# The crossing between two layers: token rows modulated in place and transposed by DMA instead of by TensorE

## The chip, the cores and the metric

The kernel runs on one core of a Trainium2 chip. Its five engines run from queues of their own and meet through semaphores: TensorE (PE, with its weight loads shown as PEld), VectorE (DVE), ScalarE (ACT), GpSimd (POOL) and SyncE (SP), whose queue issues most of the DMAs; ScalarE and GpSimd issue a few as well. The metric is the device time of one execution in microseconds. The kernel before takes 1306.46 us, the median of three runs (1306.09 to 1312.27).

## The reference, cut to what matters

One step of a two-layer backbone on 256 context ("prompt") tokens and 1024 latent tokens of width 1024. Layer 0 mixes tokens by a chunked gated linear attention (GLA), layer 1 by grouped-query softmax attention. Each layer normalises, scales and shifts its input, and adds its gated branch to it:

```
h = rms_norm(x, norm_g[l]) * (1 + sc) + sh        # sc, sh, gt: of the request, by silu(c) @ w_ada[l] + b_ada[l]
# layer 0
y = (rms_norm(o_f + flip(o_b), onorm) * silu(gate)) @ w_out
x = x + gt * y
# layer 1
q, k, v, gate = split(h @ w_in)                   # on the new x, normalised and modulated for layer 1
q = rms_norm(q, qn); k = rms_norm(k, kn)          # latent tokens: rope_2d(q), rope_2d(k)
```

Context and latent tokens have different sc, sh and gt. All products are formed in 16 bits with each factor split into a high and a low half (three products for one), so each h is needed as hi and lo, with the width on the partitions.

## The kernel before, in words

The tokens are ten tiles of 128: tiles 0 and 1 are the prompt, 2 to 9 the latent tokens. `hT_hi` and `hT_lo` hold the 16-bit halves of a layer's input, transposed: width on the partitions, tokens along the free dimension.

The GLA layer is a loop of 50 slots (`gla`): four heads over ten tiles, and ten more slots in which the last head is finished. A function `filler(slot)` hangs other work on the slots: the products with `w_ada`, the splitting of layer 1's weights, the layer's scale and shift (`affine(1)` in slot 37), the loading of w_out (slots 30 to 38). Work that shall wait for the slot's own instructions is put into `k.jobs` and run under `issue_after`. In slots 42, 44, 46 and 48 the gated outputs of tiles 2 to 5 are split and transposed by DMA into `hT` (`out_load`, `out_prep`); in slots 45 and 47 the first two output tiles are multiplied (`residual` with the banks A and kt).

`gla_out` is the crossing: it carries the tiles from layer 0 to layer 1, in the order 2 to 9, 0, 1. For each tile n from the third on: load the tile's row x, multiply the gated output with w_out (`residual`: two halves of 512 columns, each in a PSUM bank "y"; VectorE scales the bank by the gate and adds it into x), store x for the next layer (`x1_d`, by GpSimd's queue), split and transpose the gated output of the tile after next. After every second tile both x are normalised (`normalise`: squares summed by ScalarE, the power -1/2 by GpSimd, the row scaled by VectorE). While the next pair is multiplied, the finished pair is transposed by TensorE, 128 columns at a time, into PSUM banks "tr" (`transpose`); ScalarE applies scale and shift from there (`modulate`, `h`), GpSimd rounds to `hT_hi`, VectorE writes the rest to `hT_lo`. Then the pair's two key tiles are multiplied (`key_tile`, banks "kv"), normed, turned by the rotary table and transposed by DMA into `kT`. After the loop the rotary table is multiplied with the query norm (`fold_rope`), the query weights are loaded (`query_start`), two query tiles are projected, and the last pair, the prompt, is transposed and modulated. The prompt's own key tiles come in `attention`, between the score products (bank S) of its first step.

The program says what depends on what and which tile has how many buffers. The order of instructions on each engine and queue is made by the framework, which plays the program through with modelled durations and issues what is ready first; `issue_after(x)` puts a group behind instruction x on x's engine. On the chip each engine and queue then keeps that order. DMAs that transpose are all issued from SP.

Of the kernel before, what the change touches and what calls it, by code (L numbers as in the profile page):

```python
# [7 lines left out]
F16 = mybir.dt.float16  # L8
BF16 = mybir.dt.bfloat16
F32 = mybir.dt.float32  # L10
# [43 lines left out]
class K:  # L54
# [269 lines left out]
    def affine(self, l):  # L324
        nc, sp = self.nc, self.const
        mod = self.modT[l]
        g = self.t(sp, [P, KT, 2], F32, f"gs{l}")
        gT = self.gT[:, 8 * l : 8 * l + 8].unsqueeze(2).to_broadcast([P, KT, 2])
        nc.vector.scalar_tensor_tensor(g, mod[:, 8:16, :], 1.0, gT, ALU.add, ALU.mult)
        sh = self.t(sp, [P, KT, 2], F32, f"sh{l}")  # L330
# [10 lines left out]
        return g, sh, c  # L341
# [432 lines left out]
    def residual(self, i, lhs, wo, inv, x, banks=None, cuts=(512, 512), out=None):  # L774
        nc = self.nc
        g = self.gt[:, 0 if i < NTP else 1, :]
        b = 0
        for j, n in enumerate(cuts):
            ps = (banks[j] if banks else self.bank("y"))[:, 0:n]
            self.pieces(ps, lhs, wo, b, n)  # L780
            a = slice(b, b + n)
            nc.vector.scalar_tensor_tensor(ps, ps, inv, g[:, a], ALU.mult, ALU.mult)  # L782
            last = nc.vector.tensor_tensor(x[:, a], ps, x[:, a], ALU.add).ins  # L783
# [7 lines left out]
    def out_load(self, i, og=None, parts=None):  # L791
        if og is None:
            og = self.t(self.xp, [P, D], F32, "og", bufs=2)
            t = self.t(self.xp, [P, 2 * D], F16, "oghl", bufs=2)
            parts = t[:, 0:D], t[:, D:]
        self.nc.sync.dma_start(og, self.og_d[i])
        return i, og, parts

    def out_prep(self, i, og, parts):
        nc = self.nc  # L800
        mx = self.t(self.small, [P, 1], F32, "wm1")
        nc.vector.tensor_reduce(mx, og, AX.X, ALU.max, apply_absolute_value=True)
        s, inv = self.pow2(mx, cross=False)
        hi, lo = parts
        nc.scalar.activation(hi, og, AF.Copy, scale=s)
        nc.vector.scalar_tensor_tensor(lo, og, s, hi, ALU.mult, ALU.subtract)
        to = [t[:, :, i * P : i * P + P] for t in (self.hT_hi, self.hT_lo)]
        nc.sync.dma_start_transpose(to[0], hi)
        nc.sync.dma_start_transpose(to[1], lo)
        return *to, inv  # L810


    def gla_out(self, wo, early, first):
# [3 lines left out]
        done, xs = (order[0], first), []  # L817
        self.gs, self.sh, self.inv_h = self.mod1
        rows = {n: self.out_load(order[n]) for n in range(len(early), len(first) + 4)}
        ckv = self.att_load()  # L820
        for n in range(len(first), NT):
            i = order[n]
            hT, lT, inv = prep.pop(i)
            x = self.t(self.xp, [P, D], F32, "xr", bufs=4)
            nc.sync.dma_start(x, xrow(self.I, i))
            last = self.residual(i, lambda k: (hT[:, k, :], lT[:, k, :]), wo, inv, x)
            nc.gpsimd.dma_start(self.x1_d[i], x)
            with self.tc.issue_after(last):
                if n + 2 in rows:
                    prep[order[n + 2]] = self.out_prep(*rows.pop(n + 2))  # L830
            if n + 4 in range(len(early), NT):
                rows[n + 4] = self.out_load(order[n + 4])
            if done:
                t0, ys = done
                if i % 2 == 0:
                    for k in range(KT):
                        act, dve = self.modulate(self.transpose(ys, k, "tr"), k, t0)
                else:
                    for j in range(2):
                        self.key_tile(t0 + j, wkv)  # L840
                    done = None
            xs.append(x)
            if n == len(first):
                d, inv = self.ahead["kv"]
                wkv = []
                t = self.w2[1]
                for j, (hi, lo) in enumerate((
                    [t[:, :, 256:512] for t in self.nw[0:2]], (t[:, :, 0:256], t[:, :, 256:512])
# [5 lines left out]
                with self.tc.issue_after(dve.ins):  # L854
                    self.att_setup(*ckv)
                    self.key_setup(*ckv, inv)
            if i % 2 == 1:
                junk = self.t(self.xp, [P, D], F16, "junk", bufs=1)
                self.normalise(xs, junk)
                done, xs = (i - 1, xs), []  # L860
# [78 lines left out]
    def att_load(self):  # L939
# [4 lines left out]
        nc.sync.dma_start(self.qn, I["att_qnorm"].to_broadcast([P, HD]))  # L944
        self.kn = self.t(ap, [P, HD], F32, "kn")
        nc.sync.dma_start(self.kn, I["att_knorm"].to_broadcast([P, HD]))
# [88 lines left out]
    def queries_out(self, q, j):  # L1035
# [4 lines left out]
        if i >= NTP:  # L1040
            r = self.head_rms(x)
            self.rope(x, i)
        else:
            self.head_norm(x, self.qn, x)
        self.split_transpose(x, None, qT[:, j].rearrange("p i h t -> p (i h) t"), r)
# [79 lines left out]

    def query_start(self):
        d, inv = self.ahead.pop("q0")
        lo = self.t(self.wp, [P, KT, 512], F16, "wlo0")
# [3 lines left out]
        self.wg = [self.load_w("g0", (0, 2))]  # L1132
# [5 lines left out]
        self.q, self.half = {}, []  # L1138

# [113 lines left out]
def emit(ctx, tc, I, O, dbg=None, stop=None):  # L1253
# [15 lines left out]
    k.gt_d = k.t(k.dram, [2, 2, D], F32, "gt_d")  # L1269
    hp = k.pool("hp")  # L1270
# [11 lines left out]
    with ExitStack() as c:  # L1282
# [8 lines left out]
        with ExitStack() as c1:  # L1291
# [51 lines left out]
            k.gs, k.sh, k.inv_h = k.affine(0)  # L1343
# [41 lines left out]
        def filler(slot):  # L1385
# [13 lines left out]
            if slot == 37:  # L1399
                k.mod1 = k.affine(1)  # L1400
# [15 lines left out]
            if slot == 40:  # L1416
                k.jobs.append((k.fold_gate, *k.gate_load(0), [t[2] for t in wo]))
                wo[:] = [(*k.w0[0:2], 512)] + [(hi, lo, 256) for hi, lo, _ in wo[2:]]
                k.w2 = k.wtile(2)
                t = k.w2[0].rearrange("p k n -> p (k n)").bitcast(F32)  # L1420
                for n in range(2):
                    xs.append(t[:, D * n : D * n + D])
                    load(xs[n], xrow(I, NTP + n))
            if slot in PREP:
# [5 lines left out]
            if slot in EARLY:  # L1430
# [6 lines left out]
                if n == 1:  # L1437
                    k.jobs.append((k.normalise, xs, k.t(k.qkp, [P, 512], F32, "q0").bitcast(F16)))
# [7 lines left out]
    with ExitStack() as ca:  # L1446
        k.ap = k.pool("ap", ctx=ca, side="right")
        with ExitStack() as c:
# [4 lines left out]
            k.held = {t: k.bank(t) for t in ("y", "kv", "tr", "mm")}  # L1453
            k.p2_bank = "kv"
            wk = k.gla_out(wo, prep, xs)
# [109 lines left out]
```

## Time and profile before

| | |
|---|---|
| median of 3 runs | 1306.46 us |
| profiled execution, its own time | 1307.08 us |
| its span, first to last instruction | 1305.2 us |
| mean granted TensorE clock | 0.984 |
| busy: PE, DVE, ACT, POOL | 1222.4, 907.5, 713.3, 370.9 us |
| GLA layer with its filler | 0 to 581 us |
| crossing (first y product to first score product) | 581.27 to 737.51 us |
| attention | 737.51 to about 1207 us |
| last output product | to 1305.2 us |

In the profile a line such as "L129 PE MATMUL y<-whi,hT_hi" names the line of the kernel, the engine, the operation, the tile written and the tiles read; L129 is the helper that forms all three-product matmuls, so the tile written tells which stage it is: y an output tile, kv a key tile, mm a query, gate or value product, S scores, tr a transpose (L358). PE instructions are pipelined, so the time that one takes is read from start to start, and the printed duration is longer. The rows themselves are shown with the prediction.

### The profile page before, as it was taken

What the parts mean: (1) busy time and instruction counts of PE and PEld (TensorE: products, weight loads), DVE (VectorE), ACT (ScalarE), POOL (GpSimd) and SP (SyncE); (2) the same over time, 40 slices, a digit from 0 to 9 for tenths busy, and PEclk for the clock granted to TensorE, in tenths of its full rate; (3) what the DMA queues carried; (4) which work ended last, traced back from release to release, by engine and by line L of the source; (5) the groups of instructions that cost most, each with busy time, mean ns of one, the idle gap of its engine ahead of it and who ended that gap; (6) DMA issues with size and microseconds to landing.
All of it is one profiled execution on the core that took longest, in us unless ns stands there. A gap on an engine that the chain in (4) does not pass through costs nothing. (4 is left out here: it accounts for less than half of the span.)

```text
span 1305.2 us, 22423 instructions
## 1 busy us (share of the span) xinstructions
PE 1222.4 (94%) x8015; PEld 791.3 (61%) x8015; DVE 907.5 (70%) x2110; ACT 713.3 (55%) x1730; POOL 370.9 (28%) x625
## 2 busy tenths in 40 slices
PE   4899999999998998798999889999999999989998
PEld 2366666555655556566877466667666666766444
DVE  5585879777876798666664667777667577786652
ACT  3684656565655566542443566666766677673110
POOL 1132214323322244311332643342233344322000
PEclk8899999999999999899999999999999999999999
DMA  9602745554646344257643376666947747879342
GB/s 366 245 33 82 219 149 179 168 158 130 189 139 195 116 150 142 82 150 261 162 120 108 91 179 130 126 131 133 202 105 167 141 87 145 175 151 236 126 153 81
DMA packets 335792, 199.12 MB, mean 153 GB/s; under 512 B 229838, under 2 KB 320446, under 8 KB 333376
## 3 DMA queue, kind: packets, MB, share of 16 engines
q1 hardware_dynamic: 328512, 180.79, 52.9%
q0 software_dynamic: 3728, 11.55, 2.7%
q10 hardware_dynamic: 3440, 5.35, 1.1%
q8 instruction: 63, 1.03, 0.3%
q14 instruction: 49, 0.40, 0.1%
HBM read 104.31 MB, written 37.24 MB: 108 GB/s over the span
## 5 line engine op out<-in xcount | busy, mean ns | idle before, releaser
L129 PEld LDWEIGHTS <-hT_hi 128*128 128x128 f16 x1920 | 188.7, 98 | 126.3 <-issue 12.8
L129 PE MATMUL mm<-whi,hT_hi 128*128 128x512 f16 (+1 forms) x576 | 200.6, 349 | 5.5 <-ACT gx L526 4.8
L129 PE MATMUL mm<-whi,hT_lo 128*128 128x512 f16 (+1 forms) x576 | 200.7, 348 | 0.0
L129 PE MATMUL mm<-wlo,hT_hi 128*128 128x512 f16 (+1 forms) x576 | 200.7, 348 | 0.0
L1094 DVE SCALAR_TENSOR_TENSOR phl<-p,srec,phl 128x1280 f16<-128x1280 f32 (+1 forms) x80 | 108.0, 1355 | 74.3 <-POOL phl L1091 43.5
L129 PEld LDWEIGHTS <-whi 128*128 128x128 f16 x1232 | 120.5, 98 | 61.6 <-issue 3.1
L129 PE MATMUL mm<-hT_hi,whi 128*128 128x256 f16 (+1 forms) x480 | 141.3, 294 | 0.7 <-ACT rope L1014 0.7
L129 PE MATMUL mm<-hT_lo,whi 128*128 128x256 f16 (+1 forms) x480 | 141.3, 294 | 0.0
L129 PE MATMUL mm<-hT_hi,wlo 128*128 128x256 f16 (+1 forms) x480 | 141.2, 294 | 0.0
L1061 PE MATMUL S<-kT,wst 128*128 128x512 f16 (+1 forms) x624 | 124.7, 342 | 11.5 <-ACT p L1069 11.5
L129 PEld LDWEIGHTS <-hT_lo 128*128 128x128 f16 x960 | 94.5, 98 | 61.6 <-issue 1.4
L129 PE MATMUL mm<-PT,vh 128*128 128x256 f16 x672 | 113.8, 275 | 8.8 <-DMA PT<-phl 6.0
L1091 POOL TENSOR_SCALAR phl<-p,srec 128x1280 f16<-128x1280 f32 (+1 forms) x40 | 55.4, 1384 | 200.4 <-DVE srec L1085 74.2
L1064 DVE TENSOR_REDUCE smx<-S 128x1 f32<-128x1280 f32 (+1 forms) x80 | 101.5, 1268 | 11.7 <-PE S L1061 11.7
L1069 ACT ACTIVATE p<-S,snb,sexp 128x1280 f32<-128x1280 f32 (+1 forms) x80 | 99.3, 1242 | 8.6 <-DVE phl L1094 3.7
L1061 PEld LDWEIGHTS <-wst 128*128 128x128 f16 x624 | 61.6, 99 | 66.1 <-issue 15.6
L129 PE MATMUL mm<-PT,vl 128*128 128x256 f16 x336 | 92.3, 275 | 0.0
L152 DVE TENSOR_REDUCE wmx<-wst 128x1 f32<-128x512 f32 x104 | 64.7, 676 | 22.0 <-DMA wst<-in_gla_w_in 8.7
L129 PEld LDWEIGHTS <-wlo 128*128 128x128 f16 x616 | 60.3, 98 | 31.5 <-DVE wlo L1222 1.8
L129 PEld LDWEIGHTS <-vh 128*128 128x128 f16 x672 | 65.6, 99 | 19.9 <-issue 8.3
L1066 ACT ACTIVATE snb<-smx,nsexp 128x1 f32<-128x1 f32 x80 | 23.3, 291 | 85.0 <-DVE smx L1064 84.8
L901 POOL TENSOR_TENSOR rope<-hx,ropet 128x64 f32<-128x64 f32 x160 | 63.1, 424 | 18.8 <-ACT hx L1027 11.2
(358 smaller groups left out, 2724.2 us busy)
## 6 DMA issues: line engine op xcount, KB each, us to landing
wada<-in_w_ada SPq DMA_DIRECT2D x16, 1024.0 KB
wst<-in_gla_w_in SPq DMA_DIRECT2D x12, 1024.0 KB
wst<-in_att_w_in SPq DMA_DIRECT2D x10, 1024.0 KB
og_d<-gx SPq DMA_DIRECT2D x40, 128.0 KB
og_d<-og POOLq DMA_DIRECT2D x40, 128.0 KB, 2.8
wst<-og_d SPq DMA_DIRECT2D x5, 1024.0 KB
xr<-x_d SPq DMA_DIRECT2D x9, 512.0 KB
out<-xr ACTq DMA_DIRECT2D x17, 256.0 KB
```

The lines of the kernel that those rows point to most:

```text
L129: self.nc.tensor.matmul(out, a, b, start=k == 0 and j == 0, stop=k == n - 1 and j == 2)
L152: nc.vector.tensor_reduce(mx[:, j : j + 1], st[:, 2 * j : 2 * j + 2, :], AX.XY, ALU.max, apply_absolute_value=True)
L901: nc.gpsimd.tensor_tensor(tv[:, h, :, w, :], xv[:, h, :, 1 - w, :], sn[:, :, w, :], ALU.mult)
L1061: nc.tensor.matmul(S[:, a : a + n], x, y, start=m == 0, stop=m == 2)
L1064: last = nc.vector.tensor_reduce(mx, S, AX.X, ALU.max).ins
L1066: nc.scalar.activation(nb, mx, AF.Copy, scale=self.nsexp)
L1069: nc.scalar.activation(p, S, AF.Exp, scale=self.sexp, bias=nb, accum_out=den)
L1091: nc.gpsimd.tensor_scalar(hi, p, r, 2.0 ** 14, ALU.mult, ALU.mult)
L1094: nc.vector.scalar_tensor_tensor(lo, p, r2, hi, ALU.mult, ALU.subtract)
```

## The change

The modulated rows are formed with tokens on the partitions and then transposed by DMA.

- `affine(1)` writes scale and shift into one tile. It runs as a job of slot 34. A job of slot 35 (`affine_rows`) transposes this tile on TensorE into 32 rows, copies them out of PSUM and stores them as `gb_d` in DRAM. `rows_load` loads scale and shift of one request, each 1024 values, broadcast to all partitions: 512 KB each, for the latent tokens in slot 40, for the prompt before tile 0.
- `mod_tile` replaces `normalise`, `transpose` and `modulate` for a tile: squares on ScalarE, the power on GpSimd, x times the factor times the scale row on VectorE, plus the shift row in two halves, rounding to `hi` on ScalarE, the rest to `lo` on VectorE, and two transposing DMAs of 128 x 1024 into `hT`. The first two tiles have it as jobs of slots 45 and 47, the others directly behind their residual.
- There is no "tr" bank; "y" has four buffers instead of two, and the PSUM banks are taken in the order kv, mm, y.
- Key tiles come one by one: none with the first output tile of `gla_out`, one with the next, then two, then one each; the last latent key tile and the two query tiles stand ahead of the last output tile.
- The first two query tiles are normed with `qn` itself and turned by the unfolded table; the table is folded after the loop (`query_low`). The low half of the first query weights is loaded into the place of `og` for them, and once more into its old place `wlo0` afterwards.
- The second half of the key weights goes into a tile of its own (`half`). The x rows are loaded two tiles ahead, the first two of them by GpSimd's queue, and so are the two norm vectors.

```diff
     def affine(self, l):
...
-        g = self.t(sp, [P, KT, 2], F32, f"gs{l}")
+        gb = self.t(sp, [P, 2, 2, KT], F32, f"gb{l}")
+        g, sh = (gb[:, j].rearrange("p i k -> p k i") for j in range(2))
...
+    def affine_rows(self, gb):
+        ps = self.bank("mm")[0:32, 0:P]
+        self.nc.tensor.transpose(ps, gb.rearrange("p s i k -> p (s i k)"), self.ident)
+        r = self.t(self.ew, [P, 256], F32, "mod")[0:32, 0:P]
+        self.nc.vector.tensor_copy(r, ps)
+        self.nc.sync.dma_start(self.gb_d.rearrange("s i (k p) -> (s i k) p", p=P), r)
+
+    def rows_load(self, i):
+        t = self.gb.rearrange("p k n -> p (k n)").bitcast(F32)
+        self.gbr = [t[:, D * j : D * j + D] for j in range(2)]
+        for j in range(2):
+            self.nc.sync.dma_start(self.gbr[j], self.gb_d[j, i : i + 1, :].to_broadcast([P, D]))
+
+    def mod_tile(self, i, x, parts, after=None):
...
+        nc.scalar.activation(hi, x, AF.Square, accum_out=ssq)
+        r = self.rstd(ssq, D, "nt_r")
+        g, b = self.gbr
+        with ExitStack() as c:
+            if after is not None:
+                c.enter_context(self.tc.issue_after(after))
+            nc.vector.scalar_tensor_tensor(x, x, r, g, ALU.mult, ALU.mult)
+            cuts = [slice(512 * j, 512 * j + 512) for j in range(2)]
+            for a in cuts:
+                nc.vector.tensor_tensor(x[:, a], x[:, a], b[:, a], ALU.add)
+            for a in cuts:
+                nc.scalar.copy(hi[:, a], x[:, a])
+                nc.vector.tensor_tensor(lo[:, a], x[:, a], hi[:, a], ALU.subtract)
+        for t, p in ((self.hT_hi, hi), (self.hT_lo, lo)):
+            nc.sync.dma_start_transpose(t[:, :, i * P : i * P + P], p)
...
-            ps = (banks[j] if banks else self.bank("y"))[:, 0:n]
+            ps = (banks[j] if banks else self.bank("y", 4))[:, 0:n]
...
-    def gla_out(self, wo, early, first):
+    def gla_out(self, wo, early, n0):
...
+        def load(n):
+            if n < NT:
+                xs[n] = self.t(self.xp, [P, D], F32, "xr", bufs=4)
+                (nc.gpsimd if n < n0 + 2 else nc.sync).dma_start(xs[n], xrow(self.I, order[n]))
+
+        load(n0)
+        load(n0 + 1)
...
+        for n in range(n0, NT):
             i = order[n]
+            if n == NT - 1:
+                self.query_rest()
+                self.query()
+                self.key_tile(order[n - 2], wkv)
+                self.query_rest()
...
+            load(n + 2)
...
-            if done:
-                t0, ys = done
-                if i % 2 == 0:
-                    for k in range(KT):
-                        act, dve = self.modulate(self.transpose(ys, k, "tr"), k, t0)
-                else:
-                    for j in range(2):
-                        self.key_tile(t0 + j, wkv)
-                    done = None
-            xs.append(x)
+            t = self.t(self.xp, [P, 2, D], F16, "hl", bufs=2)
+            if i == 0:
+                self.rows_load(0)
+            self.mod_tile(i, x, (t[:, 0], t[:, 1]), self.last)
+            for j in {3: (0,), 4: (1, 2), 5: (3,), 6: (4,), 7: (5,), 8: (6,)}.get(n, ()):
+                self.key_tile(order[j], wkv)
+            if n == 8:
+                self.query()
...
-        self.fold_rope(self.qn)
-        self.query_start()
-        for j in range(2):
-            self.query()
-            self.query_rest()
-        t0, ys = done
-        for k in range(KT):
-            self.modulate(self.transpose(ys, k, "tr"), k, t0)
+            if n == 7:
+                self.query_start()
+        self.query_low()
...
+    def query_low(self):
+        self.fold_rope(self.qn)
+        self.folded = True
+        d, inv = self.ahead.pop("q0")
+        lo = self.t(self.wp, [P, KT, 512], F16, "wlo0")
+        self.nc.sync.dma_start(lo, d[:, 1])
+        self.wq = [((self.q0, lo, inv), self.wq[0][1])]
+        self.wg = [self.load_w("g0", (0, 2))]
...
-            if slot == 37:
-                k.mod1 = k.affine(1)
+            if slot == 34:
+                k.jobs.append((lambda: setattr(k, "mod1", k.affine(1)),))
+            if slot == 35:
+                k.jobs.append((k.affine_rows, k.mod1[0]))
...
-                if n == 1:
-                    k.jobs.append((k.normalise, xs, k.t(k.qkp, [P, 512], F32, "q0").bitcast(F16)))
+                t = k.t(k.spl, [P, 2, KT // 2, 256], F16, "split").rearrange("p j k n -> p j (k n)")
+                k.jobs.append((k.mod_tile, NTP + n, xs[n], (t[:, 0], t[:, 1])))
...
-            k.held = {t: k.bank(t) for t in ("y", "kv", "tr", "mm")}
+            k.held = {t: k.bank(t, n) for t, n in (("kv", 2), ("mm", 2), ("y", 4))}
```

More of the change, by code (lines that the diff above doesn't have):

```diff
@@ L853, in gla_out @@
                     wkv.append((hi, lo, 256))
-                with self.tc.issue_after(dve.ins):
+                with self.tc.issue_after(last):
                     self.att_setup(*ckv)
                     self.key_setup(*ckv, inv)
[L857 to L860, printed above, removed]
             if n == 4:
@@ L1039, in queries_out @@
         r = None
-        if i >= NTP:
+        if i >= NTP and self.folded:
             r = self.head_rms(x)
@@ L1044, in queries_out @@
             self.head_norm(x, self.qn, x)
+            if i >= NTP:
+                self.rope(x, i)
         self.split_transpose(x, None, qT[:, j].rearrange("p i h t -> p (i h) t"), r)
@@ L1126, in query_start @@
     def query_start(self):
-        d, inv = self.ahead.pop("q0")
-        lo = self.t(self.wp, [P, KT, 512], F16, "wlo0")
+        self.folded = False
+        d, inv = self.ahead["q0"]
+        lo = self.og.rearrange("p j n -> p (j n)").bitcast(F16).rearrange("p (k n) -> p k n", k=KT)
         self.nc.sync.dma_start(lo, d[:, 1])
```

44 lines of the change are left out of this document (24 added, 20 removed).

## The prediction, made before the result was known

> **What bounds the kernel now.** I read the busy time by stretches first, then the TensorE's timeline through the crossing, then what the other engines do beside it. The stretches (columns: length, then busy time and count of PE, PEld, DVE, ACT, POOL, the granted clock, the DMA share, GB/s):
>
> ```profile
> core 0: us, PE busy (x) PEld busy (x) DVE busy (x) ACT busy (x) POOL busy (x), PEclk, DMA share, GB/s
> 581.27:737.51 156.24, 148.22 (x1095) 108.30 (x1092) 95.54 (x234) 62.55 (x156) 47.84 (x107) 0.98 0.53 156
> 737.51:1207.50 469.99, 448.68 (x3186) 312.17 (x3185) 333.22 (x649) 308.50 (x747) 162.96 (x249) 0.99 0.72 149
> 1207.50:1305.20 97.70, 91.17 (x445) 43.10 (x443) 45.36 (x76) 8.86 (x8) 0.54 (x1) 1.00 0.34 120
> ```
>
> The crossing is the first row: PE is busy 148 of 156 us, no other engine more than 96. So the stage costs what PE has to do in it, plus the few places where PE stands. The timeline of PE shows both (start, duration, and in brackets the idle time before with its releaser):
>
> ```profile
> 581.27 0.38 PE L129 MATMUL y<-whi,hT_hi 128*128 128x512 f16 x1
> ...
> 591.69 0.60 PE L358 MATMUL tr<-ident,whi 128*128 128x128 f32 x4
> 595.99 0.58 PE L129 MATMUL y<-whi,hT_hi 128*128 128x512 f16 x1 [3.70 <-DVE xr L783]
> ...
> 602.05 0.60 PE L358 MATMUL tr<-ident,whi 128*128 128x128 f32 x4
> 602.48 0.38 PE L129 MATMUL y<-whi,hT_hi 128*128 128x512 f16 x1
> ...
> 616.94 0.27 PE L129 MATMUL kv<-whi,hT_hi 128*128 128x256 f16 x1
> ...
> 627.42 0.27 PE L129 MATMUL y<-whi,hT_lo 128*128 128x256 f16 x1
> ...
> 729.51 0.60 PE L358 MATMUL tr<-ident,xr 128*128 128x128 f32 x4
> 731.86 0.89 PE L358 MATMUL tr<-ident,xr 128*128 128x128 f32 x4 [1.74 <-ACT h L370]
> 733.82 0.44 PE L358 MATMUL tr<-ident,xr 128*128 128x128 f32 x2 [1.07 <-ACT h L370]
> 735.68 2.03 PE L358 MATMUL tr<-ident,xr 128*128 128x128 f32 x6 [1.43 <-ACT h L370]
> 737.51 2.56 PE L1061 MATMUL S<-kT,wst 128*128 128x512 f16 x9
> 739.91 0.38 PE L129 MATMUL mm<-whi,hT_hi 128*128 128x512 f16 x1
> ...
> 745.09 1.79 PE L1061 MATMUL S<-kT,wst 128*128 128x512 f16 x9
> 746.71 0.27 PE L129 MATMUL mm<-whi,hT_hi 128*128 128x256 f16 x1
> ```
>
> From start to start: a whole output tile (y) is 591.69 - 581.27 = 10.42 us; two key tiles are 627.42 - 616.94 = 10.48, so 5.24 each; a query projection (24 products of 512 columns) is 745.09 - 739.91 = 5.18, or 0.216 a product; four transposes are 602.48 - 602.05 = 0.43. Two places are lost time. At 592 PE waits 3.70 us for a y bank, and the 21 products behind it then take 602.05 - 595.99 = 6.06 instead of 4.53: 1.5 more at a lower clock. At the end the prompt tiles' 16 transposes last from 729.51 to 737.51, 8.0 us, because each waits for ScalarE to empty a tr bank; and the first S group after them takes 739.91 - 737.51 = 2.40 where the next takes 1.62, another 0.8.
>
> [...]
>
> **The change, part by part.** Removed from PE: 64 transposes among the output tiles, 16 x 0.43 = 6.9; the tail, 8.0 with its own 16; the slow first S, 0.8. Two changes lift the wait at 592: four y banks instead of two, so that PE may go on while VectorE is late, and the x row begun on the GpSimd queue, because the lateness was this:
>
> ```profile
> 589.19 0.75 DVE L782 SCALAR_TENSOR_TENSOR y<-y,p2i,wst 128x512 f32<-128x512 f32 x1
> 595.24 0.69 DVE L783 TENSOR_TENSOR xr<-y,xr 128x512 f32<-128x512 f32 x1 [5.30 <-DMA xr<-in_x_sample]
> 588.89 0.42 SPq L825 DMA_DIRECT2D xr<-in_x_sample  x1
> ```
>
> The row was issued at 588.89, behind everything else on SP, and landed 6.35 us later. Either change alone lifts PE's wait: 3.7 + 1.5 = 5.2. Together 6.9 + 8.0 + 0.8 + 5.2 = 20.9. As a check the other way round: eight y tiles, eight key tiles and two queries are 83.4 + 41.9 + 10.4 = 135.7 us of PE, so S could begin at 581.27 + 135.7 = 717.0 instead of 737.5, 20.5 earlier, and 0.8 more for the first S. I take 21.
>
> What replaces them goes to VectorE, ScalarE and the SP queue. The prices, from the groups of instructions of the crossing (busy and mean ns, then idle before):
>
> ```profile
> L375 DVE TENSOR_TENSOR hT_lo<-h,hT_hi 128x256 f16<-128x256 f32 x37 | 15.4, 443 | 6.4 <-POOL hT_hi L374 6.4
> L782 DVE SCALAR_TENSOR_TENSOR y<-y,p2i,wst 128x512 f32<-128x512 f32 x16 | 12.1, 756 | 16.1 <-PE y L129 16.1
> L783 DVE TENSOR_TENSOR xr<-y,xr 128x512 f32<-128x512 f32 x16 | 11.0, 685 | 5.4 <-DMA xr<-in_x_sample 5.3
> L806 DVE SCALAR_TENSOR_TENSOR oghl<-og,p2s,oghl 128x1024 f16<-128x1024 f32 x6 | 7.7, 1283 | 2.7 <-ACT oghl L805 2.6
> L802 DVE TENSOR_REDUCE wm<-og 128x1 f32<-128x1024 f32 x6 | 7.2, 1207 | 0.0
> L352 DVE TENSOR_SCALAR xr<-xr,nt_r 128x1024 f32<-128x1024 f32 x8 | 6.0, 751 | 4.1 <-DMA x_d<-xr 2.5 <-POOL nt_r L120 1.5
> L903 DVE TENSOR_TENSOR hx<-hx,ropet 128x256 f32<-128x256 f32 x12 | 5.4, 453 | 7.4 <-POOL rope L901 7.4
> L890 DVE SCALAR_TENSOR_TENSOR hx<-hx,hrs,kn 128x128 f32<-128x128 f32 x16 | 4.9, 349 | 6.3 <-POOL hrs L120 6.3
> L936 DVE SCALAR_TENSOR_TENSOR xhl<-hx,asc,xhl 128x256 f16<-128x256 f32 x8 | 3.9, 492 | 0.9 <-ACT xhl L935 0.9
> L1010 DVE SCALAR_TENSOR_TENSOR vl<-kv,psv,vh 128x256 f16<-128x256 f32 x8 | 3.9, 482 | 3.4 <-ACT vh L1009 3.4
> L910 DVE TENSOR_TENSOR ropet<-ropet,qn 128x1024 f32<-128x1024 f32 x1 | 1.2, 1212 | 0.0
> L98 DVE TENSOR_SCALAR p2e<-p2c 128x1 int32<-128x1 int32 x6 | 0.9, 152 | 0.2
> ```
>
> - A token tile's modulation cost VectorE 0.75 + 4 x 0.44 = 2.5 us; now one 1024-wide product (1.28), two 512-wide sums and two 512-wide differences (4 x 0.685): 4.0. With the residual (2 x 1.44 = 2.9), the next tile's split (1.21 + 1.28 + 4 x 0.15 = 3.1) and a key tile (0.48 + 2 x 0.35 + 2 x 0.45 + 0.49 + 0.15 = 2.7) VectorE has 12.7 us per tile against PE's 10.42 + 5.24 = 15.7. It stays beside PE; if that cover went, each us over 15.7 would cost 8. ScalarE and GpSimd lose work (no 256-wide copies out of tr banks, no hT_hi copies), and have more room still.
> - SP gets two more transposing DMAs per tile, beside the two of the split. It held them like this, and a store of x delayed the write in place like this:
>
> ```profile
> 601.33 1.32 SPq L808 DMA_TRANSPOSE hT_hi<-oghl  x1
> 602.75 1.59 SPq L809 DMA_TRANSPOSE hT_lo<-oghl  x1
> 650.50 0.75 DVE L352 TENSOR_SCALAR xr<-xr,nt_r 128x1024 f32<-128x1024 f32 x1 [1.48 <-DMA x_d<-xr]
> 702.97 0.33 SPq L1129 DMA_DIRECT2D wlo<-w_q  x1
> ```
>
> The next two rows are a stretch (same columns as above) and PE in the last GLA slots:
>
> ```profile
> 710.00:712.00 2.00, 2.00 (x21) 1.80 (x19) 1.32 (x4) 0.64 (x1) 0.38 (x1) 1.00 0.01 4
> 548.67 0.37 PE L129 MATMUL mm<-whi,hT_hi 128*128 128x256 f16 x1 [3.84 <-ACT gx L526]
> ```
>
>   Four of some 1.45 are 5.8 us of queue per 15.7: covered. A split's columns are wanted two tiles later, a modulated tile's at least two tiles later but for the last.
> - **Last GLA slots.** The scale moved from slot 37 to 34, one 32-row transpose (0.1), its store, two row loads of 512 KB, and two modulations moved into slots 46 and 48 in place of the joint normalise and PE work. This stretch is touchy: at 548.67 PE stood 3.84 us behind ScalarE in just this kind of job. It may gain or lose that much; I take +0.5 and keep -3.8 and +3.8.
> - **First key tile.** It moves from 616.94 to 581.27 + 2 x 10.42 = 602.1. Half of its weights went into a tile that was free in the last GLA slots; now that half goes into a tile of the crossing's own pool, so its load falls into the crossing's start, where the 512 KB of the x row took 6.35 us. Ends 0 and 6.3; I take 1.5, nearer to nothing since 20 us lie before it.
> - **The low half of the query weights** is loaded twice. The second load can start only after the last output tile's first half, and the third query wants it 5.24 + 1.62 = 6.9 later. The load of 702.97 was through before 710 (a DMA share of 0.01 in the row above), so 7.0 or less beside another of its size. I take 1, ends 0 and 7.
> - **Start of attention.** The last prompt tile's modulation (4.0) and the folding of the rotary table (1.21 + 4 x 0.45 = 3.0) now fall on VectorE after attention has begun. There it is 333/470 = 71% busy: 7.0 more in the first 20 us is 21.2. Ends 1.2 and 7.0; I take 2.5, nearer to the small end since two S buffers stand between.
> - The two queries ahead of the last output tile use the unfolded table: eight more products of 0.35 (four heads in each), covered by the 3 us that VectorE has free per tile. Key and query norms loaded on GpSimd's queue: nothing on PE's path.
>
> Sum: -21 + 0.5 + 1.5 + 1 + 2.5 = -15.5. The profiled execution took 1307.08 us (span 1305.2), 0.62 above the median of 1306.46, so the sum is taken against its own time and moved by that: 1307.1 - 15.5 - 0.6 = **1291 us**. A measurement of this kernel tells about 0.5% (6.5 us) from no change. The forecast's own range is -24.8 (every added cost nothing, the GLA stall gone) to -7: 1282 to 1299.
>
> **The rivals.**
> 1. *The wait moves to the handover.* After the last output tile come residual, square, the wait for the x store, 4.0 us of VectorE and two transposes, about 12 us; the second prompt key tile wants them after three S groups, a query and a key tile, 3 x 1.62 + 5.18 + 5.24 = 15.3. If VectorE's attention work stands ahead, or SP holds the query weights behind these transposes, PE waits up to about 9 more (7 for the load, 1.5 for the clock). For it: the 3 us of slack are small. Against: the parts are placed by readiness, as the load at 702.97 was, ahead of earlier key transposes. Time 1291 + 9 = 1300, half of it still a gain over 0.5%.
> 2. *VectorE becomes the bound, and the kernel slower.* Place: the write in place that waits for the x store, in order on VectorE, for each tile (1.48 at 650.50). With w us of such waits, 12.7 + w passes PE's 15.7 at w = 3.0; slower than before by 0.5% from (w - 3.0) x 8 > 15.5 + 6.5, w = 5.8. At w = 7 it costs 32: 1323 us. For it: one queue more to be late on and a serial chain; against: the split stands between store and write and covers 3 us.
> 3. *The transposes by DMA are too slow.* At 1.3 to 1.6 us for eight blocks SP's queue keeps up, and it would have to be 15.7 / 5.8 = 2.7 times slower to become the bound; at four times, 23 us a tile against 15.7 would cost 8 x 7.5 = 60: 1351 us. [...]
>
> **How the numbers follow.** Forecast 0.68, rival 1 0.19, rival 2 0.11, rival 3 0.02. Faster: 0.68 + half of rival 1 = 0.77; same: the rest of it, 0.10; slower: 0.13. The range takes the forecast and most of rival 1, 1282 to 1303, and leaves out rivals 2 and 3 and a twentieth of the others.
>
> **What would show it.** Right: no tr group; y tiles back to back from 581 on, PE's idle time in the crossing under 3 us; S begins near 720; VectorE near 80% between. Wrong: PE waits named DMA hT_hi or DVE xr at every tile (rivals 2 and 3); a wait on DMA wlo or hT behind the first S groups (rival 1); a longer stretch before 581, which would mean that the slots 34 to 48 lost more than the 3.8 that I allow.

## The result, and the profile after

The changed kernel takes 1306.41 us (median; 1301.02 to 1311.20) against 1306.70 us for the kernel before: a ratio of 0.9999, 95% interval 0.9988 to 1.0010. The forecast was 1291. The profiled execution has a span of 1306.6 us against 1305.2, at the same clock (0.983 and 0.984).

The stretches after, cut as in the prediction (first y product, first score product, last output product; same columns):

```profile
core 0: us, PE busy (x) PEld busy (x) DVE busy (x) ACT busy (x) POOL busy (x), PEclk, DMA share, GB/s
584.80:736.33 151.53, 139.75 (x1014) 99.92 (x1012) 106.18 (x238) 51.61 (x128) 40.97 (x79) 0.95 0.79 196
736.33:1208.50 472.17, 448.26 (x3187) 312.33 (x3185) 337.08 (x649) 310.36 (x747) 158.62 (x243) 0.99 0.74 154
```

The crossing starts 3.5 us later and is only 4.7 us shorter, where 20.5 were worked out. PE is busy in 139.75 us of it, near the 135.7 that the prediction worked out for the products alone, so the removed work is gone. The rest is standing and slow clock (0.95 granted instead of 0.98). Where PE stands, its timeline after shows:

```profile
584.80 0.38 PE L129 MATMUL y<-whi,hT_hi 128*128 128x512 f16 x1
...
598.69 0.39 PE L129 MATMUL y<-whi,hT_lo 128*128 128x512 f16 x1 [2.87 <-DMA hT_lo<-k]
...
619.44 1.01 PE L129 MATMUL mm<-whi,hT_hi 128*128 128x512 f16 x2 [8.90 <-DMA whi<-w_q]
620.35 0.41 PE L129 MATMUL kv<-whi,hT_hi 128*128 128x256 f16 x1
...
627.21 0.38 PE L129 MATMUL y<-whi,hT_hi 128*128 128x512 f16 x1
...
736.33 0.81 PE L1104 MATMUL S<-kT,wst 128*128 128x512 f16 x3
...
750.89 1.78 PE L1104 MATMUL S<-kT,wst 128*128 128x512 f16 x9 [3.02 <-ACT p L1112]
```

From 627.21 to 736.33 PE does not stand once: six y tiles, seven key tiles and two queries in 109.1 us, which is what their products cost. All of the loss lies in the first 42 us: 584.80 to 627.21 holds two y tiles and one key tile with two query products, 26.5 us of work (2 x 10.42 + 5.24 + 2 x 0.216), and takes 42.4. Of the 15.9 lost, 2.87 + 8.90 = 11.8 are two waits and about 4 the slow clock behind them. The prediction's 1.5 us for a late first key tile (ends 0 and 6.3) has no slow clock in it; here the clock is 0.50 from 619.44 to 623.00, behind the longer wait, and behind the shorter one the ten products from 599.34 on take 3.4 us at 0.51, where 0.216 us for each would be 2.2 (same columns as the stretches above):

```profile
599.30:602.70 3.40, 3.40 (x10) 1.17 (x9) 2.96 (x14) 1.15 (x2) 0.54 (x1) 0.51 1.25 216
```

What came late? SP's queue in that stretch (start, time that the entry held the queue):

```profile
586.44 1.59 SPq L845 DMA_TRANSPOSE hT_lo<-k  x1
...
590.55 0.56 SPq L902 DMA_DIRECT2D wlo<-w_kv  x1
591.21 10.09 SPq L377 DMA_TRANSPOSE hT_hi<-split  x1
...
602.00 1.58 SPq L377 DMA_TRANSPOSE hT_lo<-split  x1
...
604.86 0.92 SPq L832 DMA_DIRECT2D og<-og_d  x2
...
606.33 0.43 SPq L901 DMA_DIRECT2D wkv<-w_kv  x1
...
607.89 3.75 SPq L861 DMA_DIRECT2D xr<-in_x_sample  x1
611.68 0.43 SPq L909 DMA_DIRECT2D whi<-w_q  x1
```

The first transpose of tile 3's modulated rows held the queue 10.09 us, and all that stands behind it slipped: the gated rows of tiles 6 and 7, the second half of the key weights, the query weights that PE waits for at 619. The wait of 2.87 us is for the first row shown, tile 5's transpose, which was issued ahead of that hold and released PE 12.2 us later. VectorE stood too (first row: the x row, begun on GpSimd at 586.75, ahead of the hold as well; second row: the gated rows behind it):

```profile
598.24 0.69 DVE L819 TENSOR_TENSOR xr<-y,xr 128x512 f32<-128x512 f32 x1 [5.14 <-DMA xr<-in_x_sample]
...
609.35 1.22 DVE L838 TENSOR_REDUCE wm<-og 128x1 f32<-128x1024 f32 x1 [6.69 <-DMA og<-og_d]
```

Beside the hold stand full DMA engines. The same stretches of 6 us, before and then after (the last two columns are the DMA share and GB/s):

```profile
588.00:594.00 6.00, 4.29 (x40) 3.75 (x38) 1.58 (x3) 1.32 (x3) 0.81 (x2) 1.00 1.09 372
...
606.00:612.00 6.00, 6.00 (x45) 4.23 (x43) 3.40 (x9) 1.61 (x4) 1.88 (x4) 1.00 0.53 165
612.00:618.00 6.00, 6.00 (x45) 4.12 (x44) 5.97 (x14) 1.15 (x2) 1.30 (x2) 1.00 0.43 179
```

```profile
588.00:594.00 6.00, 6.00 (x47) 4.49 (x46) 5.07 (x11) 1.66 (x4) 0.93 (x2) 1.00 1.22 162
...
606.00:612.00 6.00, 4.54 (x42) 3.81 (x39) 2.55 (x9) 0.84 (x1) 0.56 (x1) 1.00 0.96 350
612.00:618.00 6.00, 0.00 (x0) 0.00 (x0) 5.81 (x11) 1.46 (x3) 1.14 (x2) 0.59 1.09 352
618.00:624.00 6.00, 4.56 (x25) 3.07 (x26) 3.12 (x5) 1.17 (x2) 0.00 (x0) 0.56 1.08 384
...
642.00:648.00 6.00, 6.00 (x58) 5.38 (x56) 4.93 (x9) 3.20 (x9) 1.28 (x2) 1.00 1.00 199
```

A share of 1 means that the packets' times add up to those of all 16 engines; where they overlap it passes 1, as the 1.22 here. Before, the engines were full until 606 (shares of 1.04 and 1.12 in the two slices between the rows shown) and half idle from there. After, the share is 0.96 or more in every slice from 588 to 648, though PE does not stand after 627: here full engines cost PE time only where what it wants next is still behind them. From 588 to 594 they move 162 GB/s at a share of 1.22 (64.9% from SyncE's queue, 56.7% from GpSimd's), where before they moved 372. That the full engines make the hold is argued from these rows; no run separates it from the length of SyncE's own queue. What a transpose costs them is seen where two run alone, at 684.5 to 689.4 of the changed kernel (the DMA view, in its second row: packets, MB, share of 16 engines; then half a microsecond of it as a stretch):

```profile
DMA packets 2113, 0.53 MB, mean 109 GB/s; under 512 B 2112, under 2 KB 2112, under 8 KB 2112
...
q1 hardware_dynamic: 2112, 0.52, 56.0%
```

```profile
686.50:687.00 0.50, 0.50 (x7) 0.45 (x5) 0.00 (x0) 0.00 (x0) 0.50 (x2) 1.00 1.11 211
```

56.0% of 4.9 us is 2.74 us for two: 1.37 us of all 16 engines for each, or 0.26 MB at some 190 GB/s, about half the rate of the loads (372 at a share of 1.09 in the row above). The four that the change adds around this stretch are 4 x 1.37 = 5.5 us of the engines.

### The profile page after: what moved, and what is told of

Same layout as the page of the kernel before. It is cut to its first block, busy times and chain, and to the rows that moved or that the text cites. A ratio compares the mean times of both kernels' runs of the same rounds, so it can differ in the third digit from the quotient of the medians.

```text
span 1306.6 us, 22246 instructions
## 1 busy us (share of the span) xinstructions
PE 1215.6 (93%) x7936; PEld 783.7 (60%) x7936; DVE 924.6 (71%) x2120; ACT 705.4 (54%) x1706; POOL 360.7 (28%) x594
## 5 line engine op out<-in xcount | busy, mean ns | idle before, releaser
L129 PE MATMUL mm<-wlo,hT_hi 128*128 128x512 f16 (+1 forms) x560 | 194.2, 347 | 0.0
L1104 PE MATMUL S<-kT,wst 128*128 128x512 f16 (+1 forms) x624 | 122.0, 338 | 9.9 <-ACT p L1112 8.7
L129 PE MATMUL mm<-PT,vh 128*128 128x256 f16 x672 | 114.0, 275 | 11.8 <-DMA PT<-phl 8.7
```

Of the source, the lines that this page charges most:

```text
L129: self.nc.tensor.matmul(out, a, b, start=k == 0 and j == 0, stop=k == n - 1 and j == 2)
L1104: nc.tensor.matmul(S[:, a : a + n], x, y, start=m == 0, stop=m == 2)
```

## The experiments

In the diffs, lines are cut to what the edit changes. Four theories: **A**, a load on GpSimd's queue and the transposes on SyncE's disturb each other; **B**, the 16 DMA engines are simply full, so amount and order decide, not the queue; **C**, PE's order is at fault, two query products ahead of the first key tile; **D**, the scale in slot 34 delays the last GLA slots. In the table the GLA part is taken from the eviction of one gate product (the 25th, near 470 us) to the first y product, and the crossing from there to the first score product, both on the one profiled execution. The ratio is against the kernel before, with its 95% interval.

| run | time us | ratio | GLA part | crossing | longest waits of PE in the crossing |
|---|---|---|---|---|---|
| before | 1306.7 | | 111.1 | 156.2 | 3.70 xr |
| after | 1306.4 | 0.9999 (0.9988 to 1.0010) | 113.9 | 151.5 | 8.90 w_q, 2.87 hT_lo |
| e1 rows on ScalarE | 1307.3 | 1.0000 (0.9983 to 1.0018) | 113.9 | 151.4 | 13.07 w_q |
| e2 queries later | 1308.0 | 1.0007 (0.9985 to 1.0029) | 114.0 | 151.0 | 7.12 amx, 3.40 hT_lo |
| e3 scale in slot 37 | 1304.2 | 0.9974 (0.9949 to 1.0000) | 107.2 | 154.6 | 8.50 w_q, 3.10 and 3.09 hT |
| e4 rows on SyncE | 1300.2 | 0.9945 (0.9925 to 0.9966) | 112.3 | 148.1 | 5.17 amx, 2.25 hT_lo |
| e5 tile 3 later | 1302.6 | 0.9956 (0.9934 to 0.9978) | 115.2 | 148.6 | 8.71 oghl |
| e6 e4 and e5 | 1301.9 | 0.9957 (0.9930 to 0.9983) | 115.4 | 146.8 | 9.42 oghl |
| e7 two y banks | 1308.5 | 0.9997 (0.9972 to 1.0023) | 115.3 | 152.5 | 11.14 w_q, 2.78 hT_lo |
| e8 before, rows on GpSimd | 1304.2 | 0.9968 (0.9942 to 0.9994) | 111.2 | 153.6 | 2.35 oghl |
| e9 four transposes left out | 1300.2 | 0.9941 (0.9919 to 0.9963) | 114.1 | 143.3 | 3.03 hT_lo, 1.59 amx |
| e10 e3 and e4 | 1296.5 | 0.9916 (0.9892 to 0.9941) | 107.0 | 148.8 | 9.61 amx |
| e11 order by need | 1299.5 | 0.9945 (0.9924 to 0.9965) | 107.4 | 151.0 | 6.33 p2e, 3.73 hT_lo |
| e12 rows first | 1294.0 | 0.9892 (0.9860 to 0.9923) | 108.0 | 145.0 | 7.31 oghl |

**e1, the x rows on ScalarE's queue.**

```diff
-(nc.gpsimd if n < n0 + 2 else nc.sync).dma_start(xs[n], xrow(self.I, order[n]))
+(nc.scalar if n < n0 + 2 else nc.sync).dma_start(xs[n], xrow(self.I, order[n]))
```

> The first two x rows are started on ScalarE's queue instead of GpSimd's; TensorE's order and SyncE's order stay as in the changed kernel. Theory A (a load on GpSimd's queue and the transposing DMAs on SyncE's queue slow each other): the transposes of tile 3 take about 1.3 us each instead of 10.09 and 1.58, the query weights land some 8 us earlier, TensorE's waits of 2.87 and 8.90 us go, time about 1293. Theory B (too many bytes and transposes in one window, whatever the queue): the hold and the waits stay within 2 us, time within 0.5% of 1306.5.

PE's timeline and SP's queue of this run:

```profile
621.42 1.01 PE L129 MATMUL mm<-whi,hT_hi 128*128 128x512 f16 x2 [13.07 <-DMA whi<-w_q]
```

```profile
593.20 5.42 SPq L377 DMA_TRANSPOSE hT_hi<-split  x1
...
599.34 3.68 SPq L377 DMA_TRANSPOSE hT_lo<-split  x1
```

The two transposes still hold SP for 9.1 us (11.7 after), the crossing is as long, the time the same, as B had it. GpSimd's queue is not special: A in that form is out.

**e2, the early query products held back.**

```diff
-                self.query()
+                with self.tc.issue_after(held): self.query()      # held: last product of the first key tile
```

> The two query products that stand ahead of the first key tile on TensorE are held back until that key tile is done; SyncE's order is the same. Theory C (TensorE stands in order behind the query weights, and nothing else is late there): the wait of 8.90 us goes, and with it most of the slow clock behind it, 8 to 11 us, time about 1296. Theory A and B (everything on SyncE's queue is late, the key tile's own weights and scales too): a wait of 4 to 8 us comes back at the key tile, gain under 4 us, time 1303 to 1306.

```profile
617.36 0.29 PE L87 MATMUL kv<-ident,amx 128*128 128x128 bf16 x1 [7.12 <-DVE amx L999]
```

With nothing waiting for the query weights, PE waits 7.12 us for the scale of the keys, which VectorE could not form because it stood 7.96 us for the og rows, until 609.51. C alone is out: the wait of 8.90 was only the last of several late items. The wait is the one that A and B expected (4 to 8 us); their time of 1303 to 1306 is missed by 2.

**e3, the scale back in slot 37.**

```diff
-            if slot == 34:
-                k.jobs.append((lambda: setattr(k, "mod1", k.affine(1)),))
-            if slot == 35:
+            if slot == 37:
+                k.mod1 = k.affine(1)
                 k.jobs.append((k.affine_rows, k.mod1[0]))
```

> The next layer's scale is computed in slot 37 at the old place, its rows are written right behind it; nothing else differs. Theory D (the new slot of the scale costs the last GLA slots 3.5 us): the first y tile starts at about 581.3 again and the time falls to 1303. Rival: the added transposition and the chain behind it cost the same in any slot, or the 3.5 us are given back to the late loads: the crossing starts 3.5 us earlier and ends at the same time, 1306.

The first y product starts at 574.30, not at 581.3; part of that lies ahead of the 25th eviction (467.08, against 470.86 in the kernel after), so the GLA part is the fairer measure: 107.2 against 113.9. Two successive gate evictions tell where, first in the kernel after, then in e10, which has the scale in slot 37 too:

```profile
490.99 0.47 ACT L562 ACTIVATE gx<-mm,inv_g 128x256 f32<-128x256 f32 x1
...
503.68 0.46 ACT L562 ACTIVATE gx<-mm,inv_g 128x256 f32<-128x256 f32 x1
```

```profile
494.94 0.47 ACT L562 ACTIVATE gx<-mm,inv_g 128x256 f32<-128x256 f32 x1
...
503.65 0.47 ACT L562 ACTIVATE gx<-mm,inv_g 128x256 f32<-128x256 f32 x1
```

12.69 us against 8.71. That stretch is 8.70 or 8.71 us in all six kernels without the scale in slot 34 (the two of before, e3, e10, e11, e12) and 12.48 to 12.70 in the eight with it. The kernels have other work between the two evictions, so these rows alone do not give the loss. It is read from the eviction before on (481.68 and 484.87). First a wait in the kernel after, then the two stretches, after and e10 (same columns as above):

```profile
486.92 1.22 PE L639 MATMUL U<-v,ks 128*128 128x256 f32 x2 [1.98 <-DVE ks L619]
```

```profile
481.68:503.68 22.00, 17.45 (x79) 11.06 (x78) 20.89 (x69) 12.55 (x36) 9.02 (x15) 0.84 0.21 68
```

```profile
484.87:503.65 18.78, 17.43 (x94) 10.64 (x92) 18.23 (x50) 12.41 (x38) 7.88 (x14) 1.00 0.37 120
```

The kernel after takes 3.2 us longer for fewer TensorE instructions (79 against 94): PE stands 4.55 us instead of 1.35 and has a clock of 0.84 instead of 1.00. From there to the first y product it takes 3.8 us more, for 12 instructions more (3.6 us of PE), so nearly all of the 7.0 us between 113.9 and 107.0 arise in this stretch. Which of its jobs costs how much was not tried.

D holds, and it is larger than expected, since the other GLA work of the change makes the part 3 to 4 us shorter than before (107 to 108 against 111.1). But the rival is right too: in e3 part of the gain is given back. PE waits 8.50 us for the query weights and 3.10 and 3.09 for transposes, and the crossing takes 3.1 us more (154.6). The time, 1304.2, lies between the two expectations, and its interval holds both.

**e4, all x rows on SyncE.**

```diff
-(nc.gpsimd if n < n0 + 2 else nc.sync).dma_start(xs[n], xrow(self.I, order[n]))
+nc.sync.dma_start(xs[n], xrow(self.I, order[n]))
```

> All x rows are started on SyncE; the planner then also puts the two early query products behind the first key tile. Theory A: tile 3's transposes take 1.3 us each, no wait over 1 us is left on TensorE in the first three tiles, time about 1292. Theory B: SyncE's queue gets two more loads of 512 KB, the first key tile waits for its weights as long as before, 1304 to 1309.

```profile
611.11 0.29 PE L87 MATMUL kv<-ident,amx 128*128 128x128 bf16 x1 [5.17 <-DVE amx L999]
```

Faster, and by neither theory's numbers. Tile 3's transposes hold SP 5.30 and 1.24 us instead of 10.09 and 1.58, with no rows beside them, but a wait of 5.17 for VectorE's scale of the keys stays; the first x rows are issued only at 598.71 now, on GpSimd it was 586.75. From the first y product to the first key product it is 35.6 us after, 33.5 in e2, 30.4 here: 2.1 for the order of the query products, 3.1 for the place of the rows.

**e5 and e6, tile 3's modulation behind the first loads** (e6 with the rows on SyncE as well).

```diff
-                k.jobs.append((k.mod_tile, NTP + n, xs[n], (t[:, 0], t[:, 1])))
+                if n == 0:
+                    k.jobs.append((k.mod_tile, NTP + n, xs[n], (t[:, 0], t[:, 1])))
...
+            if n == n0:
+                t = self.t(self.xp, [P, 2, D], F16, "hl", bufs=2)
+                self.mod_tile(order[1], xm, (t[:, 0], t[:, 1]), last)      # xm: x of tile 3
```

> The modulation of tile 3 and its two transposes are traced behind the first loads of the crossing instead of in the last GLA slot; the first x rows stay on GpSimd. The planner puts the og, x and key-weight loads ahead of them on SyncE and, of itself, the early query products behind the keys. Theory B (the 16 DMA engines are full from 584 to 624 us, so what stands in front on SyncE decides): the og loads are issued near 595 instead of 604.9, from the first y product to the first key product 35.6 falls to 28 to 31 us, time 1300 to 1302. Theory A (GpSimd's queue is what hurts): the x rows still share the engines with the transposes, 35 us stay, 1306.

> As the one before, and all x rows started on SyncE behind the og transposes of tile 5. Theory B: first y product to first key product 26 to 29 us, time 1295 to 1299. If the order of tile 3's transposes does not matter: as with the x rows on SyncE alone, 30.4 us and 1300.

e5 is at the edge of B's range (1302.6), and its 32.2 us to the first key product miss B's 28 to 31. With the x rows still on GpSimd the crossing is 2.9 us shorter, which A did not allow. In e6 the loads run at 410 GB/s (594 to 600) and PE has no wait left that the x rows cause (VectorE has the first at 595.67), yet PE waits 9.42 us for tile 6's transposes, queued behind 2 MB of weights and tables. B's numbers for e6 are missed (31.8 us to the first key product for 26 to 29, 1301.9 for 1295 to 1299); the time is nearer to the rival's 1300, by which the place of tile 3's transposes does not matter. Moving one item makes the next one late.

**e7 and e8, two parts of the change that were to lift the wait at 592.**

```diff
-self.bank("y", 4)          # e7: four y banks become two
+self.bank("y", 2)
...
-            nc.sync.dma_start(x, xrow(self.I, i))      # e8: in the kernel before
+            (nc.gpsimd if n < len(first) + 2 else nc.sync).dma_start(x, xrow(self.I, i))
```

> The residuals' y tile takes turns in 2 banks of PSUM instead of 4; the order on TensorE, VectorE and SyncE stays. If the two further banks carry a gain of their own: TensorE waits for VectorE's xr (598 us) within the second y tile, 2 to 5 us, and the time is 1309 to 1311. If what is late are the transposes of tile 5 and the loads behind them: that wait is swallowed by the two waits that stand there anyway, time within 0.3% of 1306.5.

> The kernel before with one part of the change: its first two x rows of the crossing are started on GpSimd. By the prediction this alone lifts TensorE's wait of 3.70 us at 592: 1301 to 1303. Theory A: with only two transposes in that window little is slowed, 1303. Theory B: the rows come no earlier, since the DMA engines are full there; within 0.3% of 1306.7.

PE's row in e7, then VectorE's and PE's in e8:

```profile
619.59 1.01 PE L129 MATMUL mm<-whi,hT_hi 128*128 128x512 f16 x2 [11.14 <-DMA whi<-w_q]
```

```profile
593.59 0.69 DVE L783 TENSOR_TENSOR xr<-y,xr 128x512 f32<-128x512 f32 x1 [0.81 <-DMA xr<-in_x_sample]
```

```profile
608.91 0.39 PE L129 MATMUL y<-whi,hT_hi 128*128 128x512 f16 x1 [2.35 <-DMA hT_hi<-oghl]
```

In the changed kernel four banks instead of two show no gain: the two waits that stand there anyway take in what they would save. Four banks in the kernel before were not tried. The early rows alone do lift the wait of 3.70 in the kernel before, as the prediction had it; 2.35 come back at 608.91, and the time is 4.2 us lower (ratio 0.9968), where the prediction charged 5.2. B missed here: by it the rows would come no earlier, but VectorE has its row 10.1 us after the first y product (593.59), against 14.0 in the kernel before (595.24).

**e9, the four transposes of the modulated tiles 2 and 3 left out** (two of eight latent key tiles are then computed from other rows).

```diff
-        for t, p in ((self.hT_hi, hi), (self.hT_lo, lo)):
+        for t, p in ((self.hT_hi, hi), (self.hT_lo, lo))[: 0 if i in (2, 3) else 2]:
```

> The four transposing DMAs of the modulated tiles 2 and 3 are left out, so these two key tiles are computed from what stands in that place; everything else is done. Theory B (full DMA engines): two transposes alone took 56.0% of 4.9 us of the 16 engines, 1.37 us each, so 5.5 us of engine time and two holds of SyncE go; from the first y product to the first key product 35.6 falls to 27 to 30 us, time 1298 to 1301. If it is the loads alone and not the transposes: 34 us or more, 1305 to 1307.

```profile
612.41 0.23 PE L87 MATMUL kv<-ident,amx 128*128 128x128 bf16 x1 [1.59 <-DVE amx L999]
```

B holds: 27.6 us from the first y to the first key product, the crossing 8.2 us shorter, 1300.2 us. Alone these transposes cost 5.5 us of the engines; among the loads they cost the crossing more than that. The run takes away their engine time and their holds of SyncE's queue together, so it does not say which of the two the crossing paid for. The framework also put the early query products behind the first key tile here; by e2 that is worth 0.5 us of crossing.

The first wait of PE is not theirs: it stays, at 3.03. It is for tile 5's transposes, the second of which is issued 1.6 us after the first y product in the changed kernel (586.44 and 584.80) and 1.3 us ahead of it in the kernel before (579.93 and 581.27). Why it comes later was not tried.

**e10, e3 and e4 together; e11 and e12, a new order on SyncE.** e11 puts tile 6's og load and transposes ahead of the second key weights, the rope table and later x rows, and the first key tile behind the third y tile. e12 instead puts the first two x rows in front, and the rope table and tile 7's x rows behind tile 6's transposes. Both have e3, e4 and e5 in them. The core of e11, then that of e12:

```diff
-            for j in {3: (0,), 4: (1, 2), 5: (3,), 6: (4,), 7: (5,), 8: (6,)}.get(n, ()):
+            for j in {4: (0, 1), 5: (2, 3), 6: (4,), 7: (5,), 8: (6,)}.get(n, ()):
...
+            with self.tc.issue_after(spt):      # spt: the second transpose of tile 6
+                load(n + 2)                     # second key weights and rope table likewise
```

```diff
         load(n0 + 1)
+        rows_ins = self.ld                      # the DMA of that x row
...
-        ckv = self.att_load()
+        with self.tc.issue_after(rows_ins):     # the key weights' loads likewise
+            ckv = self.att_load()
...
+                with self.tc.issue_after(spt):  # from the fourth tile on, load(n + 2) likewise
+                    nc.sync.dma_start(self.ropet, self.I["k_rope"])
```

> The x rows on SyncE and the scale in slot 37 together. If the two places are independent: -7.2 (rows) and -3.4 (scale) add to a ratio near 0.992, time 1296. If what the last GLA slots gain is lost again in front of the loads, as theory B has it when the loads start no earlier: ratio 0.995, 1300.

> Scale in slot 37, x rows on SyncE, tile 3's modulation behind the first loads, and an order by need on SyncE: the og load of tile 6 and its two transposes ahead of the second key weights, of the rope table and of the x rows of tiles 6 and 7; the first key tile behind the third y tile. Theory B (what stands in front on the full DMA engines decides): no wait over 3 us on TensorE in the crossing, about 10 us less than with the rows on SyncE, time 1288 to 1293. If the amount alone decides and not the order: 1297 to 1301.

> Scale in slot 37 and x rows on SyncE as in the run that has both; in addition the first two x rows stand on SyncE ahead of the caches, the key weights and tile 3's modulation, and the rope table and the x rows of tile 7 stand behind tile 6's two transposes. Theory: on the full DMA engines the x rows were the late item that held VectorE (7.89 us at 600.9) and with it the scale for the first key tile (TensorE's 9.61 us); put first, they land by about 593, TensorE's longest wait in the crossing falls under 4 us, time 1288 to 1292. Rival: the amount alone decides, and what is put behind becomes the late item; a wait of 6 to 10 us stays, on the key weights or the og transposes, 1295 to 1299.

PE's row of e11, then PE's and VectorE's of e12:

```profile
602.36 0.70 PE L87 MATMUL kv<-ident,amx 128*128 128x128 bf16 x4 [6.33 <-DVE p2e L98]
```

```profile
607.84 0.61 PE L129 MATMUL y<-whi,hT_hi 128*128 128x512 f16 x1 [7.31 <-DMA hT_hi<-oghl]
```

```profile
590.40 0.69 DVE L819 TENSOR_TENSOR xr<-y,xr 128x512 f32<-128x512 f32 x1 [2.39 <-DMA xr<-in_x_sample]
```

e10: the two places add up (1296.5). e11 misses, and its time is the one expected if the amount alone decides (1297 to 1301): the x rows stood behind a store and landed at 596.28, which held VectorE for 9.21 us and the scale again, and from 600 to 606 the DMA engines were only 40% busy while SP waited in order for tile 6. e12 is the fastest, 0.9892: VectorE waits 2.39 us for its row instead of 7.89 in e10. Its time lies between the two expectations; the wait is the rival's, 7.31 us, now on tile 6's transposes behind the key weights. So order, with tile 3's later place, is worth some 4 us of crossing (148.8 to 145.0, one profiled execution each; the intervals of the two ratios overlap); 145.0 is still 9 above the 135.7 of PE's work.

## Why the prediction was wrong

The parts of the two profiled executions add up: GLA +3.5, crossing -4.7, from the first score product to the end +2.6, together +1.4, the difference of the spans. The prediction had +0.5, -18.6 (20.1 less the key weights' 1.5) and +2.7.

- **64 transposes (6.9), the tail (8.0), the slow first S (0.8): right.** From 627.21 on nothing but y, key and query products stands on PE, back to back, to the first score product, and its first three products take 0.81 us at a granted clock of 1.00.
- **The wait at 592 (5.2): wrong.** "Either change alone lifts PE's wait": the rows do so in the kernel before (e8); for the y banks no run shows it, and in the changed kernel they bring nothing (e7). There two waits took its place, 2.87 and 8.90 us with 4 us of slow clock, 15.9 in all.
- **"Four of some 1.45 are 5.8 us of queue per 15.7: covered": the step that failed.** It priced a transpose by how long it holds SP's queue when all goes well, and for the mean tile. For the mean tile it is right: after 627 PE does not stand. But a transpose also takes 1.37 us of all 16 DMA engines, and those of tile 3 fall into the one stretch in which the engines were already full before (share 1.09 from 588 to 594), those of tile 2 stand just ahead of it. There the first of tile 3's held SP's queue 10.09 us instead of some 1.45. I read the DMA share as a mean of 0.53 over the crossing; the rows of 6 us would have shown it. e9 prices that step, engine time and holds together: 8.2 of the 13.9 us that the crossing falls short of the forecast. How the other 5.7 split is not shown; the first wait of some 3 us and the place of the x rows (e4) are among them.
- **First key tile's weights (1.5, ends 0 and 6.3): mis-sized.** Not one load but all of SP's queue was late; the first key product came at 620.35 instead of 602.1.
- **Last GLA slots (0.5, ends -3.8 and +3.8): mis-sized, inside its ends** (+3.5, of which 2.9 behind the 25th eviction). It is two opposite terms: with the scale in slot 37 the GLA part is 107.0 to 108.0 us, 3 to 4 less than before; in slot 34 it is 112.3 to 115.4.
- **Low half of the query weights (1) and start of attention (2.5): about right.** From the first score product to the end it is 567.7 us before and 569.3 on the mean of the twelve kernels that have the change, 566.7 to 573.8: +1.6, where 1 + 2.5 - 0.8 = 2.7 were charged. Which of the waits there (3.02 at 750.89) belongs to which part was not tried.
- **The range.** Its upper end of -7 is not the sum of the terms' own upper ends, which is -21 + 3.8 + 6.3 + 7 + 7 = +3.1. By the prediction's own ends the measured -0.3 was not excluded.
- **The rivals.** Rival 1 had the right sort of event, a wait that takes the place of the one removed, at the wrong end of the crossing. Rival 2 is false: no write in place holds PE after 627. Rival 3 had the right culprit at the wrong price: the transposes are not too slow for each tile, they are too many in the first 40 us. For tiles 2 and 3 TensorE may be the better place, though no run has it: at the prediction's 0.43 us for four transposes their 16 would take PE some 1.7 us, an estimate, against the 8.2 of e9.

## What to carry to other kernels

Before work is moved to DMA, read the DMA share in the stretch where it will land, in slices of a few us, and charge each transfer with engine time as well as queue time (here 1.37 us of the engines beside some 1.45 of the queue for a transpose); a mean over the stage hides a full stretch (0.53 over the crossing before, 1.09 from 588 to 594). Here the cure of one late item on SyncE's queue was the delay of the next (PE's waits of 9.42 us in e6 and 7.31 in e12), so cut or move the amount first and then order by need. A job hung on a busy slot is worth a try in each of its neighbours: here one slot or another made a difference of 5 to 7 us in that part, and of 2 to 4 us in the whole time.

## What the hardware showed that I had not expected

A transposing DMA of 128 x 1024 in 16 bits took 1.37 us of all 16 DMA engines when alone, about half the rate of plain loads (some 190 GB/s; 372 at a share of 1.09), and beside loads the sum fell lower still: 162 GB/s at a share of 1.22. A plain load held SyncE's queue for long as well as a transpose did: 10.09 us the first transpose of tile 3, 6.97 us the second key weights in e4, and 5.17 us the same load in e10, where the share was 1.04 from 600 to 606. Begun on another queue, a load came much sooner in one kernel and hardly in the other: the x row on GpSimd's queue reached VectorE 10.1 us after the first y product in the kernel before (e8), but 13.4 in the changed one (598.24 and 584.80), and 14.0 from SyncE's queue in the kernel before.
